# Gate and value products of three of four feed-forwards by Strassen's seven block products

## The chip, the cores and the metric

The kernel runs on one core of a Trainium2 chip. The metric is the device time in microseconds (us) of one execution. TensorE (PE) multiplies, VectorE (DVE) and ScalarE (ACT) work on tiles of 128 partitions, GpSimd (POOL) does a little, and SyncE (SP) issues the weight transfers. Each engine takes its instructions in the order in which the program lists them for it, and waits at an instruction until what it needs is there.

## The reference

The reference is a trunk of two layers on 512 tokens of 1024 features, in f32. Only the feed-forwards change:

```python
def rms_norm(x, w):
    xf = x.astype(jnp.float32)
    y = xf * lax.rsqrt(jnp.mean(xf * xf, axis=-1, keepdims=True) + EPS)
    return (y * w.astype(jnp.float32)).astype(x.dtype)

def swiglu_ffn(h, w_gu, w_down):
    a, b = jnp.split(h @ w_gu, 2, axis=-1)
    return (jax.nn.silu(a) * b) @ w_down
```

A layer adds half a feed-forward, a token mixer (layer 0: MLA and GLA in parallel, "even"; layer 1: stick-breaking attention, "odd"), half a second feed-forward, and a gated per-layer embedding ("ple": `x += sigmoid(rms_norm(x) W_g) * (p W_p)`). `w_gu` is 1024 by 2816 (gates 1408, values 1408) and `w_down` is 1408 by 1024. There are four feed-forwards: (1,0), (2,0), (1,1), (2,1), first the place in the layer, then the layer.

## The kernel before

The residual x lies in eight tiles x0 to x7 of 128 features by 512 tokens. For f32 accuracy every operand of a product is cut into a high part in a rounded 32-bit form and a low part that holds the rest, and a product is three matmuls: high by high, high by low, low by high (`mm3`, L320 to L322). A weight tile of 128 by 1024 is loaded by SP, its high part is cast on ACT (L221) and its low part subtracted on DVE (L222). `weight()` hands out weights in the order of a list (`plan`), keeps WR = 6 loads in flight and has WS = 3 of them split ahead of use.

`Norm.take(m)` follows each final residual tile: it scales the tile by the gain and splits it (L333 on ACT, L335 on DVE), squares it (L410 on ACT), and adds the square to a running sum (L419, `sqa`). `norm.sums()` has PE sum the squares over partitions (`pss`, L440), from which DVE and POOL make 1/rms (`v` L453, `rc` L455); `norm.row()` makes a row R of it for all partitions (`wide`, two matmuls, L483).

In `ffn` the weights are stationary and the 512 tokens move: each of 11 gate tiles A and 11 value tiles B is 8 k-tiles by 3 matmuls of 512 columns. `gated` (L561 to L565) multiplies by R, applies silu and multiplies, and splits the result g (L328). Then each of 8 output tiles takes 33 matmuls (`dn`) and is added to x. The first two products of a feed-forward are interleaved over k (`proj2`), so that PE meets x6 and x7 last; `norm.sums()` stands after them, `norm.row()` one product later.

A scheduler sets each engine's order at build time, from the order in which the code is written and its own estimates. It is fixed on the chip.

Of the kernel before, what the change touches and what calls it, by code (L numbers as in the profile page):

```python
# [18 lines left out]
P = 128  # L19
# [34 lines left out]
def _two_pi_parts():  # L54
    """2 pi, and 2**16 modulo 2 pi, cut into parts of 8 bits (the last one is the rest)."""
# [53 lines left out]
def tile_kernel(ctx: ExitStack, tc: tile.TileContext, a: dict, out: bass.AP):  # L109
# [156 lines left out]
    # ---- constants and inputs  # L266
# [48 lines left out]
    # ---- pieces  # L315
# [41 lines left out]
    def proj2(w0, w1, rhs, p):  # L357
        """Two products, for whose last operand there is more time."""
# [8 lines left out]
    class Filler:  # L367
        """Work for the tensor engine, to be laid between the steps of a chain."""
# [95 lines left out]
    def diagonals(cols, eng=dve):  # L464
        """Columns of tokens, in two parts, on the diagonals of blocks."""
# [13 lines left out]
    def widen(ms):  # L479
        """The diagonals as a row of the tokens on all partitions (PSUM)."""  # L480
# [12 lines left out]
    def start(norm):  # L493
        """The first two products, along with the arrival of their operands."""
# [63 lines left out]

    def gated(A, B, R, g):
# [203 lines left out]
    def values(keys, xn, done):  # L763
        """Values of 4 heads, tokens on partitions."""
# [13 lines left out]
    def even_mixer(norm, nxt, cos, sin):  # L778
# [131 lines left out]
        # decays from exact sums of the logs, of two kinds at a time  # L910
# [19 lines left out]
        # weights of the pairs within a block: [j, (block, head of the pair), i]; the diagonal first  # L930
# [23 lines left out]
        # operands of the levels; the two heads' queries stand apart, zeros in the other's rows  # L954
# [5 lines left out]
        # states between blocks  # L960
# [90 lines left out]
        # the rotated key, for the heads on either half of the quadrants  # L1051
# [162 lines left out]
    # the place of a block of keys in the banks of a head's scores, for the queries from it on  # L1214
# [3 lines left out]
    def odd_mixer(norm, nxt):  # L1218
# [32 lines left out]
        def scores(h):  # L1251
# [19 lines left out]
            # sums over the later blocks of keys  # L1271
# [100 lines left out]
    for l in range(DEPTH):  # L1372
        last = l == DEPTH - 1
        nxt = Norm(G_MIX + KD * l)
        ffn(1, l, norm, nxt, begun=begun if l == 0 else None, during=during if l == 0 else None)
        norm, nxt = nxt, Norm(G_FFN2 + KD * l)
# [6 lines left out]
        ffn(  # L1383
# [88 lines left out]
```

## Time and profile before

| | |
|---|---|
| median of 3 runs (1325.88 to 1328.06 us) | 1326.98 us |
| profiled execution: span | 1327.2 us |
| busy: PE, DVE, ACT, POOL | 1304.0, 733.5, 541.4, 138.1 us |
| mean granted TensorE clock | 0.990 |
| longest sums of PE's waits: for DVE's xnl, for DVE's mq | 6.7 us, 5.4 us |

The profiled execution's own time is its span from first to last instruction; nothing measurable lies around it, since it is 0.2 us above the median of the runs. Busy time is the time in which at least one of an engine's instructions is under way. Matmuls overlap, so a matmul's duration is longer than its distance to the next one; the distance (pitch) is what a row of them costs. The clock is a share of full speed: 1.00 is 2.4 GHz, 0.50 is 1.2 GHz.

### The profile page before, as it was taken

To read this page: it belongs to the slowest core of one execution; us is meant where nothing else is said; L and a number is where in the kernel's file an instruction comes from. 1 tells how busy PE (TensorE), PEld (TensorE's weight loads), DVE (VectorE), ACT (ScalarE), POOL (GpSimd) and SP (SyncE) were. 2 spreads that over 40 slices of the span, in tenths; PEclk is the share of its full clock that TensorE was granted. 3 is DMA by queue.
4 is the path that set the end of the run, shared out by engine and by line. 5 is a ranking of instruction groups with operands and counts; after the bars stand their busy time and mean duration, and the time that the engine had idled before them with its cause. 6 is when DMAs were issued, how large, how long until landed. Compare 5 with 4: busy or idle time off the path is not lost.

```text
span 1327.2 us, 15466 instructions
## 1 busy us (share of the span) xinstructions
PE 1304.0 (98%) x6086; PEld 1089.4 (82%) x6086; DVE 733.5 (55%) x1059; ACT 541.4 (41%) x848; POOL 138.1 (10%) x148
## 2 busy tenths in 40 slices
PE   7999999998999999999999999999999999999997
PEld 5888888887888888888888888888888888888886
DVE  6575443579865544454664444444767555444544
ACT  4333333333643333243543223334778533223442
POOL 4200000425450000000100000000111000000000
PEclk8999999998999999999999999999999999999999
DMA  7432233112301232233333223322113023323411
GB/s 237 124 96 75 85 126 106 50 44 66 109 1 48 96 95 81 83 112 113 91 108 96 86 69 100 128 95 96 64 64 97 15 84 108 96 76 103 140 47 63
DMA packets 38008, 118.59 MB, mean 89 GB/s; under 512 B 4455, under 2 KB 5608, under 8 KB 37936
## 3 DMA queue, kind: packets, MB, share of 16 engines
q1 hardware_dynamic: 36576, 114.64, 27.6%
q0 software_dynamic: 640, 1.89, 0.5%
q8 instruction: 47, 0.77, 0.2%
q10 hardware_dynamic: 720, 1.09, 0.2%
q14 instruction: 25, 0.20, 0.1%
HBM read 115.50 MB, written 2.10 MB: 89 GB/s over the span
## 4 chain that ended last, share of the span: by engine, by line
PE 92%; DVE 4%; issue 1%; ACT 1%; POOL 0%; POOLq 0%
PE A L321 6%; PE A L322 6%; PE A L320 6%; PE dn L320 6%; PE dn L321 6%; PE dn L322 6%; PE B L321 6%; PE B L320 6%; PE B L322 5%; PE sqk L320 2%; PE sqk L322 2%; PE sqk L321 2%; PE val L773 2%; PE val L775 2%; PE val L774 2%
## 5 line engine op out<-in xcount | busy, mean ns | idle before, releaser
L221 ACT CAST wh<-wr 128x1024 fp32r<-128x1024 f32 (+3 forms) x223 | 211.2, 949 | 546.9 <-issue 197.5
L222 DVE TENSOR_TENSOR wl<-wr,wh 128x1024 fp32r<-128x1024 f32 (+3 forms) x223 | 251.9, 1132 | 138.2 <-ACT wh L221 137.9
L321 PE MATMUL A<-xnl,wh 128*128 128x512 f32 x376 | 148.3, 394 | 6.7 <-DVE xnl L335 6.7
L320 PE MATMUL A<-xnh,wh 128*128 128x512 f32 x376 | 148.3, 394 | 0.1
L322 PE MATMUL A<-xnh,wl 128*128 128x512 f32 x376 | 147.6, 393 | 0.0
L320 PE MATMUL dn<-gh,wh 128*128 128x512 f32 x352 | 137.0, 389 | 0.0
L322 PE MATMUL dn<-gh,wl 128*128 128x512 f32 x352 | 137.0, 389 | 0.0
L321 PE MATMUL dn<-gl,wh 128*128 128x512 f32 x352 | 136.9, 389 | 0.0
L320 PE MATMUL B<-xnh,wh 128*128 128x512 f32 x328 | 128.3, 391 | 0.0
L322 PE MATMUL B<-xnh,wl 128*128 128x512 f32 x328 | 128.2, 391 | 0.0
L321 PE MATMUL B<-xnl,wh 128*128 128x512 f32 x328 | 128.2, 391 | 0.0
L321 PEld LDWEIGHTS A<-xnl,wh 128*128 128x128 f32 x376 | 71.3, 190 | 24.4 <-DVE xnl L335 10.0
L564 DVE TENSOR_TENSOR bb<-B,R 128x512 f32<-128x512 f32 x41 | 28.3, 690 | 108.3 <-PE B L322 108.3
L455 POOL TENSOR_TENSOR rc<-v,half 128x4 f32<-128x4 f32 x8 | 11.9, 1486 | 713.4 <-DVE v L453 713.4
L320 PEld LDWEIGHTS A<-xnh,wh 128*128 128x128 f32 x376 | 71.3, 190 | 15.7 <-ACT wh L221 0.8
L322 PEld LDWEIGHTS A<-xnh,wl 128*128 128x128 f32 x376 | 71.2, 189 | 14.6
L322 PEld LDWEIGHTS dn<-gh,wl 128*128 128x128 f32 x352 | 66.1, 188 | 13.8
L320 PEld LDWEIGHTS dn<-gh,wh 128*128 128x128 f32 x352 | 66.1, 188 | 13.7
L321 PEld LDWEIGHTS dn<-gl,wh 128*128 128x128 f32 x352 | 66.1, 188 | 13.6
L321 PEld LDWEIGHTS B<-xnl,wh 128*128 128x128 f32 x328 | 62.0, 189 | 13.0
L322 PEld LDWEIGHTS B<-xnh,wl 128*128 128x128 f32 x328 | 61.9, 189 | 13.0
L320 PEld LDWEIGHTS B<-xnh,wh 128*128 128x128 f32 x328 | 61.9, 189 | 13.0
(380 smaller groups left out, 2501.5 us busy)
## 6 DMA issues: line engine op xcount, KB each, us to landing
wr<-in_gu SPq DMA_DIRECT2D x86, 512.0 KB, 3.5
wr<-in_dn SPq DMA_DIRECT2D x32, 384.0 KB, 3.0
wr<-in_dn SPq DMA_DIRECT2D x32, 320.0 KB, 2.9
wr<-in_od_qk SPq DMA_DIRECT2D x16, 512.0 KB, 3.2
wr<-in_ev_in SPq DMA_DIRECT2D x12, 512.0 KB, 3.5
wr<-in_ev_out SPq DMA_DIRECT2D x8, 512.0 KB, 3.7
wr<-in_pg SPq DMA_DIRECT2D x8, 512.0 KB, 3.2
wr<-in_od_v SPq DMA_DIRECT2D x8, 512.0 KB, 3.2
```

The costliest lines, as they stand in the source:

```text
L221: act.copy(hi[:, cs], t[:, cs])
L222: dve.tensor_tensor(lo[:, cs], t[:, cs], f32(hi)[:, cs], op=ALU.subtract)
L320: pe.matmul(acc, wh, xh, start=start, stop=False, **k)
L321: pe.matmul(acc, wh, xl, start=False, stop=False, **k)
L322: pe.matmul(acc, wl, xh, start=False, stop=stop, **k)
L455: pool.tensor_tensor(r, v, half[:, :n], op=ALU.pow)
L564: dve.tensor_mul(b, B, R)
L773: pe.matmul(accs[b], xn[k][0][:, bs], wh[:, ws], start=k == 0, stop=False)
L774: pe.matmul(accs[b], xn[k][0][:, bs], wl[:, ws], start=False, stop=False)
L775: pe.matmul(accs[b], xn[k][1][:, bs], wh[:, ws], start=False, stop=k == KD - 1)
```

## The change

Three feed-forwards, all but (1,0), take `ffn7` and `Norm7`. Tokens are cut into two halves of 256, features into even and odd tiles, and the columns of `w_gu` into gates and values; so h @ w_gu is a product of 2 by 2 blocks, done with seven block products in place of eight. It goes in three groups of columns (512, 512 and 384 of the gates, with the same of the values). In a group each product is 24 matmuls: 2 blocks of 128 tokens, 4 k-tiles, 3 parts. The activations are stationary and the weights move, as many columns as the group has.

- **Weights.** The raw blocks of a group are 8 loads of 128 by 1024 (128 by 768 in the third). Four of the seven products need a difference of blocks: `w_term` subtracts in place on DVE (L268), 8 subtractions a group, and each of the 14 halves ("units") is then split as before (cast on ACT L247, subtraction on DVE L248). WS is 4, WR is 8 for grouped weights and 5 for others.
- **Activations.** `Norm7.take` makes the same differences of the normed activations: for an even tile two scaled copies on ACT, one subtraction of 256 tokens on DVE (`nv`, L504) and a split; for an odd tile a scaled split (`no`), `nu` (L513, L514), `nw` (L515), a split of `nu` and one of half `nw` (L521). The squares and their sum stay (now L462, L471).
- **After the products.** The sums (`al`, `be`, `ga` in PSUM, two banks each) are copied by ACT and added by DVE (`add`, L693). `close` applies silu with 1/rms as a scale per token (tokens lie on partitions now) and multiplies (L699). PE turns each of the 11 result tiles back with 4 transposes of 128 by 128 (`turn`, `gT`), and they are split. R and `wide` are not made.
- **Order.** `norm.sums()` is called after the first product (B11), ahead of the second (B21).

```diff
+        if by_seven(w, l):
+            for g in range(len(GROUPS)):
+                plan.extend(("sg", w, l, g, t, u) for t in TERMS for u in range(2))
+        else:
...
+    loads, needs, done = [], [], []
+    base, grouped = {}, set()
+    for key in plan:
+        over = done[-1] if done else 0
+        if key[0] != "sg":
+            loads.append(source(key))
+            needs.append(len(loads))
+            done.append(over + 1)
+            continue
+        g = key[:4]
+        if g not in base:
+            base[g] = len(loads)
+            grouped.update(range(len(loads), len(loads) + 8))
+            _, w_, l_, g_ = g
+            n = 2 * GROUPS[g_]
+            src = a[f"sg{w_}"][l_, g_] if GROUPS[g_] == S else a[f"sh{w_}"][l_]
+            loads.extend((src[b, u], n) for b in range(4) for u in range(2))
+        needs.append(base[g] + LAST_NEED[key[4]] * 2 + key[5] + 1)
+        done.append(over + FREED.get(key[4], 0))
...
+    def w_term(key):
+        _, _, _, _, term, u = key
+        b0 = base[key[:4]]
+        (b11, n), (b21, _), (b12, _), (b22, _) = [raw.get(b0 + 2 * b + u, (None, 0)) for b in range(4)]
+        sub = lambda o, x, y: dve.tensor_tensor(o[:, :n], x[:, :n], y[:, :n], op=ALU.subtract)
+        if term == "T1":
+            sub(b11, b12, b11)
+        elif term == "T2":
+            sub(b11, b22, b11)
+        elif term == "T3":
+            sub(b12, b22, b12)
+        elif term == "T4":
+            sub(b21, b21, b11)
+        return {"B11": b11, "B21": b21, "T1": b11, "T2": b11, "B22": b22, "T3": b12, "T4": b21}[term], n
...
+        if plan[i][0] == "sg":
+            t, n = w_term(plan[i])
+            ready[i] = w_tiles()
+            w_cut(t, n, *ready[i], slice(0, n))
+            at[1] += 1
+            return
...
-        while at[0] < min(at[2] + 1 + WR, len(plan)):
-            w_load()
-        while at[1] < min(at[0], at[2] + WS):
-            w_split()
+        while True:
+            of = done[at[1] - 1] if at[1] else 0
+            if at[0] < len(loads) and at[0] - of < (WR if at[0] in grouped else WR_PLAIN):
+                w_load()
+            elif at[1] < len(plan) and at[1] < at[2] + WS and needs[at[1]] <= at[0]:
+                w_split()
+            else:
+                break
...
+    class Norm7(Norm):
+        def __init__(self, col):
+            super().__init__(col)
+            self.even, self.odd, self.both, self.last = [], [], [], []
+            self.kept = None
+        def take(self, m, eng=dve):
+            g = gain(self.col + m)
+            lo, hi = slice(0, H), slice(H, S)
+            if m % 2 == 0:
+                v, e = sl("nv"), sl("ne")
+                act.activation(v[:, lo], x[m][:, lo], AF.Copy, scale=g)
+                act.activation(e[:, lo], x[m][:, hi], AF.Copy, scale=g)
+                dve.tensor_tensor(v[:, hi], v[:, lo], e[:, lo], op=ALU.subtract)
+                self.even.append(split(v, "nv"))
+                self.kept = v, e
+            else:
+                self.odd.append(split_scaled(x[m], g, "no"))
+                v, e = self.kept
+                u, w = sl("nu"), self.w if m % 4 == 3 else sl("nw")
+                self.w = w
+                ws = hi if m % 4 == 3 else lo
+                dve.scalar_tensor_tensor(u[:, lo], x[m][:, hi], g, e[:, lo], op0=ALU.mult, op1=ALU.add)
+                dve.tensor_tensor(u[:, hi], u[:, lo], v[:, lo], op=ALU.subtract)
+                dve.scalar_tensor_tensor(w[:, ws], x[m][:, lo], g, u[:, hi], op0=ALU.mult, op1=ALU.subtract)
+                self.both.append(split(u, "nu"))
+                if m % 4 == 1:
+                    self.last.append((sl("nwh", F32R), sl("nwl", F32R)))
+                h, l = self.last[-1]
+                act.copy(h[:, ws], w[:, ws])
+                dve.tensor_tensor(l[:, ws], w[:, ws], f32(h)[:, ws], op=ALU.subtract)
+            self.square(m, eng)
+        def side(self, term, j):
+            if term in ("B11", "T3"):
+                return self.even[j], H * (term == "T3")
+            if term in ("B21", "T4"):
+                return self.odd[j], H * (term == "T4")
+            if term in ("T1", "T2"):
+                return self.both[j], H * (term == "T2")
+            return self.last[j // 2], H * (j % 2)
...
+    def ffn7(w, l, norm, nxt, during=None, after=None):
+        g, turning = [], []
+        def product(accs, gi, term, first, last):
+            n = GROUPS[gi]
+            units = [weight("sg", w, l, gi, term, u) for u in range(2)]
+            for t in range(2):
+                for j in range(KD // 2):
+                    (h, lw), c = norm.side(term, j)
+                    cs = slice(c + t * P, c + t * P + P)
+                    wh, wl = units[j // 2]
+                    ws = slice((j % 2) * n, (j % 2) * n + n)
+                    o = accs[t][:, :n]
+                    begin, end = first and j == 0, last and j == KD // 2 - 1
+                    pe.matmul(o, h[:, cs], wh[:, ws], start=begin, stop=False, skip_group_check=True)
+                    pe.matmul(o, h[:, cs], wl[:, ws], start=False, stop=False, skip_group_check=True)
+                    pe.matmul(o, lw[:, cs], wh[:, ws], start=False, stop=end, skip_group_check=True)
+        def turn(count):
+            for _ in range(min(count, len(turning))):
+                tiles, i = turning.pop(0)
+                pt = bank("gT")
+                for b in range(NB):
+                    pe.transpose(pt[:, b * P : b * P + P], tiles[b][:, i * P : i * P + P], ident)
+                g.append(split(pt, "g"))
+        def copies(accs, n):
+            out_ = [sl("r") for _ in range(2)]
+            for t in range(2):
+                act.copy(out_[t][:, :n], accs[t][:, :n])
+            return out_
+        def add(tiles, accs, n):
+            for t in range(2):
+                dve.tensor_tensor(tiles[t][:, :n], accs[t][:, :n], tiles[t][:, :n], op=ALU.add)
+        def close(c, o, srcs, b0, n):
+            for t in range(2):
+                r = rc[:, b0 + t : b0 + t + 1]
+                act.activation(c[t][:, :n], srcs[t][:, :n], AF.Silu, scale=r)
+                dve.scalar_tensor_tensor(o[t][:, :n], o[t][:, :n], r, c[t][:, :n], op0=ALU.mult, op1=ALU.mult)
+        for gi, n in enumerate(GROUPS):
+            two = lambda name: [bank(name) for _ in range(2)]
+            al = two("al")
+            product(al, gi, "B11", True, False)
+            if gi == 0:
+                rc = norm.sums()
+            c11 = copies(al, n)
+            turn(2)
+            be = two("be")
+            product(be, gi, "B21", True, True)
+            add(c11, be, n)
+            turn(2)
+            ga = two("ga")
+            product(ga, gi, "T1", True, False)
+            c22 = copies(ga, n)
+            product(al, gi, "T2", False, False)
+            c12 = copies(al, n)
+            product(ga, gi, "B22", False, True)
+            add(c12, ga, n)
+            close(c11, c12, c11, 0, n)
+            product(al, gi, "T3", False, False)
+            add(c22, al, n)
+            product(al, gi, "T4", False, True)
+            s2 = [sl("r") for _ in range(2)]
+            close(s2, c22, al, 2, n)
+            turning.extend(([*c12, *c22], i) for i in range(n // P))
...
+        cut = DN[0] // P
+        early = KF - GROUPS[-1] // P
+        accs = [bank("dn"), None]
+        part(accs[0], weight("dn", w, l, 0, 0), 0, cut, 0)
+        w01 = weight("dn", w, l, 0, 1)
+        part(accs[0], w01, cut, early, cut)
+        turn(2)
+        accs[1] = bank("dn")
+        part(accs[1], weight("dn", w, l, 1, 0), 0, cut, 0)
+        turn(2)
+        part(accs[0], w01, early, KF, cut)
...
-        ffn(1, l, norm, nxt, begun=begun if l == 0 else None, during=during if l == 0 else None)
-        norm, nxt = nxt, Norm(G_FFN2 + KD * l)
+        if by_seven(1, l):
+            ffn7(1, l, norm, nxt)
+        else:
+            ffn(1, l, norm, nxt, begun=begun if l == 0 else None, during=during if l == 0 else None)
+        norm, nxt = nxt, Norm7(G_FFN2 + KD * l)
         if l % 2 == 0:
             even_mixer(norm, nxt, *tables)
         else:
             odd_mixer(norm, nxt)
         norm, nxt = nxt, Norm(G_PLE + KD * l)
         pT = []
-        ffn(
+        ffn7(
...
-            norm, nxt = nxt, Norm(G_FFN1 + KD * (l + 1))
+            norm, nxt = nxt, Norm7(G_FFN1 + KD * (l + 1))
...
-NSLAB = 66
-WR = 6
-WS = 3
+NSLAB = 64
+WR = 8
+WR_PLAIN = 5
+WS = 4
...
+GROUPS = (512, 512, 384)
+TERMS = ("B11", "B21", "T1", "T2", "B22", "T3", "T4")
+LAST_NEED = {"B11": 0, "B21": 1, "T1": 2, "T2": 3, "B22": 3, "T3": 3, "T4": 3}
+FREED = {"T3": 2, "T4": 2}
...
+def by_seven(w, l):
+    return (w, l) != (1, 0)
```

The first place is PE's program at the start of feed-forward (2,0), where `nvh`, `nvl` are the parts of the even tiles, `noh`, `nol` those of the odd ones, `wh`, `wl` those of a weight, and `pss` the squares' sums. After the change it reads:

```order
L673 MATMUL al_3687<-wh_3596,nvh_3631 128x512
L674 MATMUL al_3687<-wl_3597,nvh_3631 128x512
L673 MATMUL al_3688<-wh_3596,nvh_3631 128x512
L674 MATMUL al_3688<-wl_3597,nvh_3631 128x512
L675 MATMUL al_3687<-wh_3596,nvl_3633 128x512
L675 MATMUL al_3688<-wh_3596,nvl_3633 128x512
L538 MATMUL pss_3722<-ones,sqa_3685 128x2
L538 MATMUL pss_3722<-ones,sqa_3685 128x2 x3
L673 MATMUL be_3735<-wh_3639,noh_3412 128x512
```

Before, PE's rows at the same place were these:

```order
L322 MATMUL A_3647<-xnh_3565,wl_3576 128x512
L320 MATMUL A_3625<-xnh_3605,wh_3535 128x512
L321 MATMUL A_3625<-xnl_3607,wh_3535 128x512
L322 MATMUL A_3625<-xnh_3605,wl_3536 128x512
L320 MATMUL A_3647<-xnh_3605,wh_3575 128x512
L321 MATMUL A_3647<-xnl_3607,wh_3575 128x512
L322 MATMUL A_3647<-xnh_3605,wl_3576 128x512
L440 MATMUL pss_3675<-ones,sqa_3611 128x2
L440 MATMUL pss_3675<-ones,sqa_3611 128x2 x3
L320 MATMUL A_3690<-xnh_3383,wh_3615 128x512
```

`pss` stood after two products (A_3625, A_3647) and now stands after one (al_3687 and al_3688 are the two token blocks of B11), ahead of all of B21.

The second place is DVE's program that leads to that `pss`: the last twelve rows up to the last sum of squares (`sqa_3685`, which `pss` reads; x7 is x_79). After:

```order
L380 TENSOR_TENSOR nvl_3633<-nv_3626,nvh_3631 128x512
L268 TENSOR_TENSOR wr_2692<-wr_2692,wr_2688 128x1024
L471 TENSOR_TENSOR sqa_3637<-sqa_3594,sq_3635 128x512
L248 TENSOR_TENSOR wl_3739<-wr_2690,wh_3738 128x1024
L387 SCALAR_TENSOR_TENSOR nol_3671<-x_79,gains,noh_3669 128x512
L513 SCALAR_TENSOR_TENSOR nu_3673<-x_79,gains,ne_3627 128x256
L268 TENSOR_TENSOR wr_2690<-wr_3504,wr_2690 128x1024
L514 TENSOR_TENSOR nu_3673<-nu_3673,nv_3626 128x256
L268 TENSOR_TENSOR wr_3297<-wr_3297,wr_2690 128x1024
L515 SCALAR_TENSOR_TENSOR nw_3580<-x_79,gains,nu_3673 128x256
L380 TENSOR_TENSOR nul_3679<-nu_3673,nuh_3677 128x512
L471 TENSOR_TENSOR sqa_3685<-sqa_3637,sq_3683 128x512
```

Before, the last rows up to `sqa_3611` were these, two whole tiles of the residual:

```order
L488 TENSOR_TENSOR x_78<-x_78,eo_3539 128x512
L222 TENSOR_TENSOR wl_3576<-wr_3413,wh_3575 128x1024
L335 SCALAR_TENSOR_TENSOR xnl_3567<-x_78,gains,xnh_3565 128x512
L419 TENSOR_TENSOR sqa_3571<-sqa_3531,sq_3569 128x512
L488 TENSOR_TENSOR x_79<-x_79,eo_3579 128x512
L222 TENSOR_TENSOR wl_3616<-wr_3453,wh_3615 128x1024
L335 SCALAR_TENSOR_TENSOR xnl_3607<-x_79,gains,xnh_3605 128x512
L419 TENSOR_TENSOR sqa_3611<-sqa_3571,sq_3609 128x512
```

Between the last residual and the last square there were 2 rows; now there are 18, with four weight subtractions (L268) and three weight splits (L248) among them. From the residual of x3 (x_75) to the last square DVE has 50 rows: 15 of 1024 columns (7 splits, 8 subtractions), 18 of 512 with two tiles, 3 of 512 with a gain, and 14 of 256. At the start of (2,1) there are likewise 50 from the residual of x4: 11, 18, 3 and 18.

The third place is ACT's program ahead of feed-forward (1,1), in the ple of layer 0, where `gt` of L794 is the sigmoid of a tile:

```order
L247 CAST wh_5545<-wr_5121 128x1024
L794 ACTIVATE gt_5418<-gt_5418 128x512
L502 ACTIVATE nv_5423<-x_76,gains 128x256
L503 ACTIVATE ne_5424<-x_76,gains 128x256
L247 CAST wh_5599<-wr_5168 128x1024
L378 CAST nvh_5428<-nv_5423 128x512
L462 ACTIVATE sq_5432<-x_76 128x512
L247 CAST wh_5604<-wr_5117 128x1024
L794 ACTIVATE gt_5472<-gt_5472 128x512
```

The casts of weights, which wait for PE to release a buffer, stand among the links of the chain of x4 (x_76) and x5. DVE's program from the first `gt` of this ple to the last square has 74 rows: 17 of 1024 (9 splits, 8 subtractions), 34 of 512 with two tiles, 4 of 512 with a gain, 19 of 256.

## Rows read from the trace of the kernel before

**Rows 1.** The page's first part: busy time by engine, share of the span, instructions.

```profile
PE 1304.0 (98%) x6086; PEld 1089.4 (82%) x6086; DVE 733.5 (55%) x1059; ACT 541.4 (41%) x848; POOL 138.1 (10%) x148
```

**Rows 2.** The page's chain that ended last, by engine.

```profile
PE 92%; DVE 4%; issue 1%; ACT 1%; POOL 0%; POOLq 0%
```

**Rows 3.** PE's waits: engine, line and waited for; total us, times, longest.

```profile
PE A L321 <- DVE xnl L335: 6.7, 5, 2.6
PE pa L1030 <- DVE mq L1021: 5.4, 3, 3.0
```

**Rows 4.** Windows: us, busy PE PEld DVE ACT POOL (instructions), clock, DMA share, GB/s.

```profile
446.00:624.00 178.00, 178.00 (x791) 147.44 (x790) 87.56 (x112) 60.45 (x80) 1.94 (x1) 1.00 0.32 101
...
416.00:456.00 40.00, 40.00 (x182) 33.19 (x181) 19.96 (x29) 14.29 (x18) 1.94 (x1) 1.00 0.28 93
640.00:686.00 46.00, 46.00 (x209) 38.20 (x208) 31.95 (x41) 22.19 (x32) 9.70 (x6) 1.00 0.25 80
1058.00:1095.00 37.00, 37.00 (x169) 30.75 (x168) 23.46 (x35) 16.41 (x23) 1.94 (x1) 1.00 0.25 76
```

**Rows 5.** PE's timeline, products of 512 columns; start and duration in us.

```profile
458.24 0.39 PE L320 MATMUL A<-xnh,wh 128*128 128x512 f32 x1
...
463.68 0.39 PE L320 MATMUL B<-xnh,wh 128*128 128x512 f32 x1
```

**Rows 6.** PE's timeline, matmuls of 384 columns in the even mixer.

```profile
365.28 0.33 PE L320 MATMUL sc<-krh,qrh 128*128 128x384 f32 x1
...
365.80 0.22 PE L1116 MATMUL sc<-cr 128*128 128x128 f32 x1
```

**Rows 7.** Transposes: PE's timeline, then the tile's durations (ns, least/mean/most).

```profile
1230.92 2.04 PE L608 MATMUL xt<-ident,x 128*128 128x128 f32 x16
1232.71 0.48 PE L320 MATMUL dn<-gh,wh 128*128 128x512 f32 x1
...
L608 PE MATMUL xt<-ident,x x32: 272/273/327, 1230.9 to 1283.5; 128*128 128x128 f32 x32
```

**Rows 8.** DVE's timeline ahead of feed-forward (2,0).

```profile
414.32 1.23 DVE L222 TENSOR_TENSOR wl<-wr,wh 128x1024 fp32r<-128x1024 f32 x1 [0.17 <-ACT wh L221]
415.46 0.75 DVE L335 SCALAR_TENSOR_TENSOR xnl<-x,gains,xnh 128x512 fp32r<-128x512 f32 x1
416.13 0.68 DVE L419 TENSOR_TENSOR sqa<-sqa,sq 128x512 f32<-128x512 f32 x1
...
446.89 0.16 DVE L453 TENSOR_SCALAR v<-pss 128x4 f32<-128x4 f32 x1 [8.27 <-PE pss L440]
```

**Rows 9.** DVE's timeline in the ple of layer 0, first and last tile.

```profile
635.47 0.68 DVE L595 TENSOR_TENSOR gt<-G,R 128x512 f32<-128x512 f32 x1
636.85 0.69 DVE L597 TENSOR_TENSOR gt<-gt,J 128x512 f32<-128x512 f32 x1 [0.70 <-ACT gt L596]
...
672.83 0.68 DVE L595 TENSOR_TENSOR gt<-G,R 128x512 f32<-128x512 f32 x1
673.43 1.22 DVE L222 TENSOR_TENSOR wl<-wr,wh 128x1024 fp32r<-128x1024 f32 x1
...
676.77 0.75 DVE L335 SCALAR_TENSOR_TENSOR xnl<-x,gains,xnh 128x512 fp32r<-128x512 f32 x1 [0.79 <-ACT xnh L333]
```

**Rows 10.** PE's timeline there: end of `wide`, and the first product of (1,1).

```profile
633.74 0.40 PE L320 MATMUL G<-xnh,wh 128*128 128x512 f32 x1
...
671.86 0.39 PE L320 MATMUL A<-xnh,wh 128*128 128x512 f32 x1
```

**Rows 11.** DVE groups by shape: busy us, mean ns, idle before.

```profile
L1269 DVE SCALAR_TENSOR_TENSOR u<-z,u 128x256 f32<-128x256 f32 x8 | 3.4, 420 | 1.6 <-ACT u L1267 1.6
L222 DVE TENSOR_TENSOR wl<-wr,wh 128x1024 fp32r<-128x1024 f32 x149 | 185.3, 1245 | 91.8 <-ACT wh L221 91.5
```

**Rows 12.** Windows across the even mixer's wait of PE; columns as in Rows 4.

```profile
312.00:318.00 6.00, 1.90 (x12) 1.27 (x10) 5.91 (x5) 0.00 (x0) 5.51 (x5) 0.95 0.00 0
318.00:324.00 6.00, 5.85 (x18) 4.98 (x19) 5.39 (x14) 2.23 (x4) 1.29 (x1) 0.50 0.17 59
```

More of the change, by code (lines that the diff above doesn't have):

```diff
@@ L140, in ffn_plan @@
     def ffn_plan(w, l):
-        for f in range(KF):
-            plan.append(("gu", w, l, f))
-            plan.append(("gu", w, l, KF + f))
+        if by_seven(w, l):
+            for g in range(len(GROUPS)):
+                plan.extend(("sg", w, l, g, t, u) for t in TERMS for u in range(2))
+        else:
+            for f in range(KF):
+                plan.append(("gu", w, l, f))
+                plan.append(("gu", w, l, KF + f))
         for m in range(KD):
@@ L235, in wc @@
         return w[o // S][:, o % S : o % S + P] if isinstance(w, list) else w[:, o : o + P]
+    def w_term(key):
[12 more added lines that the diff above has]
+        return {"B11": b11, "B21": b21, "T1": b11, "T2": b11, "B22": b22, "T3": b12, "T4": b21}[term], n
     def w_split():
         i = at[1]
-        t, n = raw.pop(i)
+        if plan[i][0] == "sg":
[4 more added lines that the diff above has]
+            return
+        t, n = raw.pop(needs[i] - 1)
         if kept(i):
@@ L253, in weight @@
         assert plan[at[2]] == key, (plan[at[2]], key)
-        while at[0] < min(at[2] + 1 + WR, len(plan)):
-            w_load()
-        while at[1] < min(at[0], at[2] + WS):
-            w_split()
+        while True:
[6 more added lines that the diff above has]
+                break
         k = plan[min(at[1], len(plan) - 1)][0]
         for _ in range(BURST.get(k, 0)):
-            if at[1] < min(at[0], at[2] + AHEAD) and kept(at[1]):
+            if at[1] < at[2] + AHEAD and at[1] < len(plan) and needs[at[1]] <= at[0] and kept(at[1]):
                 w_split()
@@ L555, in ffn, with part @@
             residual(m, acc, 0.5, nxt)
+            if after and m in after:
+                after[m]()
+    def ffn7(w, l, norm, nxt, during=None, after=None):
[60 more added lines that the diff above has]
+            turning.extend(([*c12, *c22], i) for i in range(n // P))
+        if during:
+            during()
+        def part(acc, wt, k0, k1, c0):
+            wh, wl = wt
+            for kk in range(k0, k1):
+                o = slice((kk - c0) * P, (kk - c0) * P + P)
+                mm3(acc, wh[:, o], wl[:, o], g[kk][0], g[kk][1], kk == 0, kk == KF - 1)
+        cut = DN[0] // P
[9 more added lines that the diff above has]
+        part(accs[0], w01, early, KF, cut)
+        for m in range(KD):
+            if m > 1:
+                accs.append(bank("dn"))
+                part(accs[m], weight("dn", w, l, m, 0), 0, cut, 0)
+            if m > 0:
+                part(accs[m], weight("dn", w, l, m, 1), cut, KF, cut)
+            residual(m, accs[m], 0.5, nxt)
@@ L1387, in tile_kernel @@
             nxt,
-            during={KF - 1: lambda: pT.extend(load_p(l))},
+            during=lambda: pT.extend(load_p(l)),
             after={3: lambda: turn_x(0, xt)} if last else None,
@@ L1421, in _layout, with groups @@
     )
+    o["gu1"] = _tiles(i["ffn1_w_gu"][0])[None]
+    def groups(w, c0, n):
+        w = w.reshape(KD // 2, 2, P, 2, FF)[..., c0 : c0 + n]
+        return w.reshape(2, 2, 2, P, 2, n).transpose(4, 2, 0, 3, 1, 5).reshape(4, 2, P, 2 * n)
     for f in (1, 2):
-        o[f"gu{f}"] = np.stack([_tiles(w) for w in i[f"ffn{f}_w_gu"]])
+        ws = i[f"ffn{f}_w_gu"]
+        o[f"sg{f}"] = np.stack([np.stack([groups(w, S * g, S) for g in range(2)]) for w in ws])
+        o[f"sh{f}"] = np.stack([groups(w, 2 * S, FF - 2 * S) for w in ws])
         o[f"dn{f}"] = np.stack([_tiles(w) for w in i[f"ffn{f}_w_down"]])
@@ L1452, in build @@
     import concourse.bacc as bacc
-    nc = bacc.Bacc("TRN2", target_bir_lowering=False, num_devices=1)
+    nc = bacc.Bacc("TRN2", target_bir_lowering=False, num_devices=1, dynamic_dma_scratch_size=4096)
     a = {
```

3 lines of the change are left out of this document (2 added, 1 removed).

## The prediction

> **What bounds the kernel now.** I read the busy times first: PE is busy 1304.0 of 1327.2 us, DVE 55% and ACT 41% of the span [rows 1]. Then the chain that ended last: 92% of it is PE, 4% DVE [rows 2]. Then PE's waits: the two longest sums are 6.7 and 5.4 us [rows 3]. So TensorE bounds the kernel, and a matmul taken away is worth its pitch, as long as nothing else makes PE wait. Then windows: in feed-forward (2,0) PE is busy in all of 178 us at clock 1.00, while DVE is busy in 87.56 and ACT in 60.45; and at the starts of the three feed-forwards that the change touches PE does not wait either, while DVE is busy 19.96 of 40, 31.95 of 46 and 23.46 of 37 us [rows 4]. So none of the waits of [rows 3] is there to be won back, and the reserve that the change draws on is DVE's.
>
> **PE, products.** From the first matmul of one product to the first of the next is 463.68 − 458.24 = 5.44 us for 24 matmuls of 512 columns, 0.2267 each [rows 5]. Three matmuls of 384 columns take 365.80 − 365.28 = 0.52, 0.173 each [rows 6], so a shorter moving side pays in proportion, with stationary operands that are new each time. A feed-forward has 22 × 24 = 528 of the first kind for gates and values: 119.7 us. After, two groups of 7 × 24 = 168 take 76.2, the third, of 384 columns, 29.1; together 105.3. That is −14.4 a feed-forward. The two `wide` matmuls go: −0.45.
>
> **PE, turning back.** 11 tiles by 4 transposes are added. 16 transposes took 1.79 us from the first to the matmul behind them, 0.112 each, though each lasts 272 ns by itself [rows 7], since they overlap. 44 × 0.112 = +4.9. The net is −14.4 − 0.45 + 4.9 = −9.9 (unrounded), three times −29.8. This alone would give 1297.4.
>
> **DVE and ACT within the groups.** DVE has 14 splits and 8 subtractions of 1024 columns in a group of 512, 10 operations of 512 with two tiles and 4 with a scale. The distances on DVE are 415.46 − 414.32 = 1.14 and 416.13 − 415.46 = 0.67 [rows 8], and 0.60 from the last `gt` to the next row [rows 9]; so 25.1 + 6.0 + 2.7 = 33.8 us, against PE's 7 × 5.44 + 16 × 0.112 = 39.9. It fits, at 85%. I cost it at nothing; cover gone, it would cost what the third rival says. The weights' bytes are unchanged, so transfers (0.32 of the engines busy [rows 4]) stay hidden.
>
> **The starts.** Here the reserve is too small. `pss` stands in PE's program ahead of all of B21, needs the last sum of squares, and everything on PE is queued behind it. Before, DVE had two rows between the last residual and that sum and then waited 8.27 us for `pss` [rows 8]. Now PE comes there one product earlier, and DVE has the additions of `Norm7` and the first group's subtractions and splits in its queue ahead of it. I sum DVE's queue at these distances, with 0.34 for 256 columns (420 ns [rows 11] less the 0.08 by which 512 columns follow closer than their 0.68 [rows 9]).
>
> (2,0): x3 becomes final at 0, x7 four products later at 21.8, and B11 ends at 27.2. DVE's 50 rows from there on are 15 × 1.14 + 18 × 0.60 + 3 × 0.67 + 14 × 0.34 = 34.7. At least 7.5 us of waiting.
>
> (1,1): from the end of `wide` PE needs 671.86 − 633.74 = 38.1 to the feed-forward [rows 10], and 43.6 to the end of B11. DVE starts 1.7 after `wide` [rows 9, 10] and has 74 rows: 17 × 1.14 + 34 × 0.60 + 4 × 0.67 + 19 × 0.34 = 48.9, done at 50.7. At least 7.1.
>
> (2,1): from x4's residual three products and B11, 21.8. DVE's 50 rows: 11 × 1.14 + 18 × 0.60 + 3 × 0.67 + 18 × 0.34 = 31.5. At least 9.7.
>
> These 24.3 us are a floor: DVE never waits in them. It will. In the ple each tile's sigmoid costs DVE a wait of 0.70 for ACT, and each scaled copy 0.79 [rows 9]; before, they fell in DVE's spare time. Eight tiles: 11.9. And the last two tiles of each start are a chain through ACT (the copies `nv` and `ne`, `nvh`, `noh`, `nuh`), while the split of a later unit also waits for PE to let go of B11's second unit: five hand-overs at 0.70, 3.5 a start. So 11.0, 22.5 and 13.2: 46.7 us. The other end is from durations in place of distances (1.245 [rows 11], 0.68, 0.75 [rows 8, 9], 0.42): 39.1, 55.3 and 35.7 for the three queues, 15.1 us more. I take 46.7, since DVE runs these rows back to back, where distances count.
>
> **The clock.** In the one place where PE idled for about 4 us, its granted clock in the next 6 us was 0.50, the level of 1.2 GHz [rows 12]. 5.85 us of work at half speed lose 2.9. I take 2.0 for each start, 6.0 in all, with 0 and 8.8 as ends.
>
> **Sum.** 1327.2 − 29.8 + 46.7 + 6.0 = 1350.1. The profiled execution stands 0.2 above the median of 1326.98, which I leave out: 1350 us, 1.7% slower.
>
> **The rivals.**
> *DVE keeps ahead.* If the last square is ready when PE ends B11, the gain stays whole: 1297, faster. For it: DVE idles 2 us or more of every product of the mixers' ends now, and was 8.27 us early [rows 8]. Against it: the sums above overrun without a single wait of DVE. It decides from the point at which the three starts' waits and the slow clock behind them together are under 27 us (0.2%, 2.7 us, is about what a measurement of this kernel can tell from no change).
> *The floor alone.* DVE runs without hand-overs: 24.3, and 0 to 6 for the clock: 1322 to 1328, at the edge between faster and the same. It wants ACT never to be late, while ACT gets the `Norm7` copies as well, and casts that wait for PE stand ahead of the sigmoids in its queue.
> *DVE becomes the bound in all groups too.* If ten hand-overs of 0.79 in a group are not hidden, DVE needs 33.8 + 7.9 = 41.7 against 39.9: 1.8 in each of six groups, and in the third ones about 31.3 against 30.4, 0.9 each: 14 us more, 1364. For it: 85% on an engine that waits in order. Against it: four units are split ahead, a margin of about two products.
> *Transposes cost their duration.* 132 × 0.272 = 35.9 in place of 14.8 [rows 7]: 21 more, 1371. Against it is the row itself: the matmul behind the sixteen starts 1.79 us after the first, and no idle time stands ahead of it. The Trainium skill, page "TensorE: Matmul & The Clock Gate", section "Part 4: PE-mode transpose", gives about 275 ns for a 128 by 128 transpose in a kernel's context and says that the full clock doesn't engage for transposes. The trace agrees with the 275 as a duration (272) but not as a price.
>
> **How the numbers follow.** The forecast, waits of 36 to 60 us, gets 0.62 (its own range is 1338 to 1364); a smaller overrun (1328 to 1338) 0.06; the floor 0.10, half of it faster and half the same; DVE ahead 0.06; DVE bound in the groups 0.13; transposes 0.03. Faster is 0.06 + 0.05 = 0.11, the same 0.06 (the other half of the floor and what touches it), slower 0.83. The range reaches down into the floor, 1325, and up to 1368, the sum with the upper ends of the starts and of the clock (1327.2 − 29.8 + 61.8 + 8.8 = 1368.0); some 0.10 is left out below and 0.07 above.
>
> **What would show it.** Right: PE waits at L538 `pss` for DVE `sqa`, three times, 7 us or more each, the longest ahead of (1,1); shorter waits for `nvl` (L675) just ahead of it; DVE nearly full in the 30 to 50 us before; clock below 1.00 behind each wait; and PE full from B21 on to the end of each feed-forward, with 5.44 us a product and about 0.45 for four transposes. Wrong: no wait at `pss`; or waits of PE in the middle of groups for `wl` of L248; or transposes at 0.27. The forecast fails above all if DVE's queue runs without its hand-overs to ACT.

## The result, and the profile after

The changed kernel takes 1355.49 us (median of 4 runs, 1353.65 to 1356.53) against 1327.52 for the kernel before beside it: a ratio of 1.0216, 95% interval 1.0204 to 1.0229. It is slower by 2.2%; the forecast was 1350, range 1325 to 1368. A run's time stands above its span, by 1.8 to 3.5 us in all runs listed here (1356.53 and 1354.5 for the profiled one), so it does not hold that nothing measurable lies around the span. The prediction's sum starts from a span; its 1350.1 is therefore to be held against 1354.5.

The page of the profile after, where it answers to [rows 1, 2]: PE has 16 us less work, DVE 147 more, the span is 1354.5 us, the mean clock 0.971.

```profile
PE 1288.4 (95%) x6140; PEld 1088.7 (80%) x6140; DVE 880.9 (65%) x1242; ACT 639.4 (47%) x1010; POOL 136.9 (10%) x148
...
PE 88%; DVE 8%; ACT 2%; issue 1%; POOL 0%; POOLq 0%; DVEq 0%; ACTq 0%
```

PE's waits after, beside [rows 3]:

```profile
PE al L673 <- ACT nvh L378: 23.5, 4, 12.1
PE pss L538 <- DVE sqa L471: 17.6, 3, 7.7
...
PE al L675 <- DVE nvl L380: 1.1, 1, 1.1
```

42.2 us in eight waits, all of them between the start of a feed-forward and its `pss`. PE's timeline of the three starts (start and duration, then in brackets the idle time ahead):

```profile
435.12 0.39 PE L673 MATMUL al<-wh,nvh 128*128 128x512 f32 x1
...
442.07 0.50 PE L673 MATMUL al<-wh,nvh 128*128 128x512 f32 x1 [2.70 <-ACT nvh L378]
...
452.04 1.87 PE L538 MATMUL pss<-ones,sqa 128*128 128x2 f32 x8 [7.66 <-DVE sqa L471]
...
675.98 0.39 PE L673 MATMUL al<-wh,nvh 128*128 128x512 f32 x1
...
680.72 0.50 PE L675 MATMUL al<-wh,nvl 128*128 128x512 f32 x1 [1.12 <-DVE nvl L380]
694.04 0.80 PE L673 MATMUL al<-wh,nvh 128*128 128x512 f32 x1 [12.12 <-ACT nvh L378]
704.63 1.87 PE L538 MATMUL pss<-ones,sqa 128*128 128x2 f32 x8 [7.66 <-DVE sqa L471]
...
1099.76 0.39 PE L673 MATMUL al<-wh,nvh 128*128 128x512 f32 x1
...
1104.30 0.50 PE L673 MATMUL al<-wh,nvh 128*128 128x512 f32 x1 [1.65 <-ACT nvh L378]
1113.43 0.79 PE L673 MATMUL al<-wh,nvh 128*128 128x512 f32 x1 [7.05 <-ACT nvh L378]
1118.59 1.87 PE L538 MATMUL pss<-ones,sqa 128*128 128x2 f32 x8 [2.23 <-DVE sqa L471]
```

Undisturbed, `pss` would stand 5.44 us after the first `al`. It came 11.5, 23.2 and 13.4 us after that: 48.1 in all, of which 42.2 idle and the rest matmuls of B11 at half clock. ACT is named as the releaser of the first matmul that reads x6: it casts `nvh` from `nv`, which DVE makes. DVE's timeline at (2,0), from the residual of x3 to the last square, shows the queue that the prediction summed, with 2.2 us of idle time in 37.6:

```profile
414.35 0.68 DVE L586 TENSOR_TENSOR x<-x,eo 128x512 f32<-128x512 f32 x1
...
430.94 0.68 DVE L586 TENSOR_TENSOR x<-x,eo 128x512 f32<-128x512 f32 x1
...
439.81 1.23 DVE L248 TENSOR_TENSOR wl<-wr,wh 128x1024 fp32r<-128x1024 f32 x1 [0.85 <-ACT wh L247]
440.95 0.42 DVE L504 TENSOR_TENSOR nv<-nv,ne 128x256 f32<-128x256 f32 x1
441.28 1.22 DVE L268 TENSOR_TENSOR wr<-wr,wr 128x1024 f32<-128x1024 f32 x1
...
451.30 0.69 DVE L471 TENSOR_TENSOR sqa<-sqa,sq 128x512 f32<-128x512 f32 x1
```

The residual of x6 was final at 431.6, and `nv` of x6 began at 440.95. Weight splits and subtractions stood ahead of it on DVE, but ACT was late too: its two copies of x6, which `nv` reads, ended at 440.58, behind a weight cast that had waited for PE.

```profile
438.73 1.05 ACT L247 CAST wh<-wr 128x1024 fp32r<-128x1024 f32 x1 [1.21 <-PE al L675]
439.68 0.50 ACT L502 ACTIVATE nv<-x,gains 128x256 f32<-128x256 f32 x1
440.09 0.49 ACT L503 ACTIVATE ne<-x,gains 128x256 f32<-128x256 f32 x1
```

So the 2.70 us ahead of x6 are not DVE's alone. With DVE's order as it is, ACT's lateness can have moved the last square at (2,0) by no more than DVE's idle time, 2.2 of the 37.6 us.

The clock (windows, columns as in [rows 4]): 0.50 while PE waits, and still 0.50 for the first matmuls behind `pss`.

```profile
444.00:452.00 8.00, 0.38 (x1) 0.00 (x0) 7.35 (x12) 4.01 (x7) 0.00 (x0) 0.50 0.00 0
...
454.00:456.00 2.00, 2.00 (x5) 1.57 (x6) 0.11 (x1) 0.00 (x0) 1.01 (x1) 0.50 0.00 0
456.00:458.00 2.00, 2.00 (x8) 1.60 (x7) 0.00 (x0) 0.00 (x0) 0.00 (x0) 0.79 0.00 0
458.00:460.00 2.00, 2.00 (x10) 1.65 (x9) 0.69 (x1) 0.93 (x1) 0.00 (x0) 1.00 0.00 0
```

By stretches the balance closes. From one stage's first matmul to the next's, (2,0) became 4.0 us longer, (1,1) 15.8, (2,1) 7.1, together 26.9 of the spans' 27.3. With 9.9 won in each, 13.9, 25.7 and 17.0 were lost; 48.1 of these 56.6 stand ahead of `pss`, the other 8.5 are slow clock behind it (from its first matmul to the next product's, B21 took 6.99, 6.99 and 8.15 us in place of 5.44, and `pss` is longer too).

### The profile page after: what moved, and what is told of

It reads as the page before. It is cut to its first block, busy times and chain, and to the rows that moved or that the text cites. A ratio compares the mean times of both kernels' runs of the same rounds, so it can differ in the third digit from the quotient of the medians.

```text
span 1354.5 us, 15990 instructions
## 1 busy us (share of the span) xinstructions
PE 1288.4 (95%) x6140; PEld 1088.7 (80%) x6140; DVE 880.9 (65%) x1242; ACT 639.4 (47%) x1010; POOL 136.9 (10%) x148
## 4 chain that ended last, share of the span: by engine, by line
PE 88%; DVE 8%; ACT 2%; issue 1%; POOL 0%; POOLq 0%; DVEq 0%; ACTq 0%
PE dn L374 6%; PE dn L373 6%; PE dn L372 6%; PE al L675 4%; PE al L673 4%; PE al L674 4%; PE ga L673 2%; PE ga L675 2%; PE ga L674 2%; PE sqk L372 2%; PE sqk L374 2%; PE sqk L373 2%; PE val L971 2%; PE val L972 2%; PE val L973 2%; PE A L373 1%
## 5 line engine op out<-in xcount | busy, mean ns | idle before, releaser
L247 ACT CAST wh<-wr 128x1024 fp32r<-128x1024 f32 (+3 forms) x283 | 264.9, 938 | 418.6 <-PE dn L373 79.7
L248 DVE TENSOR_TENSOR wl<-wr,wh 128x1024 fp32r<-128x1024 f32 (+3 forms) x283 | 314.0, 1112 | 188.0 <-ACT wh L247 187.2
L268 DVE TENSOR_TENSOR wr<-wr,wr 128x1024 f32<-128x1024 f32 (+1 forms) x72 | 80.9, 1138 | 0.1
L673 PE MATMUL al<-wh,nvh 128*128 128x512 f32 (+1 forms) x144 | 55.1, 383 | 23.5 <-ACT nvh L378 23.5
L372 PEld LDWEIGHTS dn<-gh,wh 128*128 128x128 f32 x352 | 66.1, 188 | 13.4
L675 PE MATMUL al<-wh,nvl 128*128 128x512 f32 (+1 forms) x144 | 55.0, 384 | 1.3 <-DVE nvl L380 1.1
L674 PE MATMUL al<-wl,nvh 128*128 128x512 f32 (+1 forms) x144 | 54.3, 378 | 0.0
L372 PE MATMUL sqk<-xnh,wh 128*128 128x512 f32 x128 | 50.3, 393 | 0.0
L374 PE MATMUL sqk<-xnh,wl 128*128 128x512 f32 x128 | 50.0, 391 | 0.0
L373 PE MATMUL sqk<-xnl,wh 128*128 128x512 f32 x128 | 50.0, 390 | 0.0
L373 PE MATMUL A<-xnl,wh 128*128 128x512 f32 x88 | 36.0, 409 | 6.3 <-DVE xnl L387 6.3
L971 PE MATMUL val<-wh,xnh 128*128 128x512 f32 x96 | 37.6, 392 | 0.0
```

Of the source, the lines that this page charges most:

```text
L247: act.copy(hi[:, cs], t[:, cs])
L248: dve.tensor_tensor(lo[:, cs], t[:, cs], f32(hi)[:, cs], op=ALU.subtract)
L268: sub = lambda o, x, y: dve.tensor_tensor(o[:, :n], x[:, :n], y[:, :n], op=ALU.subtract)
L372: pe.matmul(acc, wh, xh, start=start, stop=False, **k)
L373: pe.matmul(acc, wh, xl, start=False, stop=False, **k)
L374: pe.matmul(acc, wl, xh, start=False, stop=stop, **k)
```

## The experiments

The theory: DVE's in-order queue is too long in the 30 to 60 us ahead of each first product, and `pss`, put ahead of B21, makes PE wait for its last entry. The rivals: only the place of `pss`; ACT's queue; DVE short of time everywhere. Every kernel is the changed one with the edit shown; line numbers shift by a few. Ratios are to the kernel before (95% intervals).

**One start less.** Feed-forward (1,1) and the norm ahead of it as before the change.

```diff
-            norm, nxt = nxt, Norm7(G_FFN1 + KD * (l + 1))
+            norm, nxt = nxt, Norm(G_FFN1 + KD * (l + 1))
...
-    return (w, l) != (1, 0)
+    return w == 2
```

> The changed kernel, with feed-forward (1,1) as before the change (and the plain norm ahead of it); (2,0) and (2,1) stay by seven products. Theory (each start costs by itself): (1,1) was 15.8 us longer than before the change (9.9 won, 20.9 waited, the rest slow clock), so 1355.5 - 15.8 = about 1340. Rival (the cost lies in things common to all three, loads and buffers): the loss halves or less, 1345 to 1350.

1337.62 us (1.0092, 1.0070 to 1.0113), 17.9 less. The waits at the other two starts stayed as they were (2.70, 7.66; 1.66, 7.05, 2.23). Each start costs by itself.

**The sums later.**

```diff
             product(al, gi, "B11", True, False)
-            if gi == 0:
-                rc = norm.sums()
...
             product(ga, gi, "B22", False, True)
+            if gi == 0:
+                rc = norm.sums()
```

> The sums of squares over partitions are asked for after the fifth product (B22) and no longer after the first; DVE's work is the same. Theory (DVE's queue is late, PE idles only because its next work stands behind it): x7's last part still comes at the same time, but PE fills the wait with B21 and most of T1; the three waits shrink from 42.2 us to about 17 (1, 13, 2) and the slow clock behind them from 14.5 to about 5: about 1320 us. Rival 1 (the place of the sums is the whole cause): only the waits at the sums go, 17.6 us, with their clock: about 1333. Rival 2 (DVE has no reserve left, the wait moves on to the weights' splits of T1 and T2): 1345 to 1355.

1324.78 us (0.9981, 0.9971 to 0.9991): 31 us from one moved call. The waits at the starts are 0.9, 9.5 and 6.0, 16.4 in all; DVE's work is unchanged (876.6 us busy). With `pss` out of the way the scheduler put half to three quarters of B21 ahead of B11's last k-tile, and the first matmuls of T1 ahead of B21's last, so more than the waits at `pss` went: the first rival's 1333 is passed. The largest part of what is left lies at (1,1), behind the ple:

```profile
672.53 0.50 PE L673 MATMUL be<-wh,noh 128*128 128x512 f32 x1 [1.76 <-ACT noh L385]
678.76 0.79 PE L673 MATMUL ga<-wh,nuh 128*128 128x512 f32 x1 [3.71 <-DVE gt L793]
690.63 0.63 PE L673 MATMUL be<-wh,noh 128*128 128x512 f32 x1 [3.68 <-ACT noh L385]
```

**Less in DVE's queue.** The first group's subtractions are pinned in program order, behind the split traced just before them. In DVE's order one of them stays ahead of the last square at each start; the others are behind it.

```diff
-        sub = lambda o, x, y: dve.tensor_tensor(o[:, :n], x[:, :n], y[:, :n], op=ALU.subtract)
+        held = tc.keep_in_program_order if key[3] == 0 else lambda i: i
+        sub = lambda o, x, y: held(dve.tensor_tensor(o[:, :n], x[:, :n], y[:, :n], op=ALU.subtract))
```

> The eight weight subtractions of each first group are kept behind the last sum of squares in DVE's order; the sums stay after the first product. Theory: 9.1, 9.1 and 6.8 us of subtractions and the two or three splits that hang on them leave DVE's queue ahead of the sums; waits fall from 10.4, 20.9 and 10.9 to about 1, 11 and 4, the clock's loss to about 5: about 1320 us, and no new wait of PE at the splits of T1. Rival (the subtractions filled gaps of DVE, which waits for ACT and PE anyway): 1350 to 1355. Rival (T1's weights come late instead): waits of 3 to 5 us appear ahead of T1 in each of the three: about 1335.

1337.16 us (1.0075, 1.0058 to 1.0092): 18 less than the changed kernel, where 35 was expected. The waits are 2.7, 15.9 and 7.5, against 1, 11 and 4. The direction holds, so the subtractions did not merely fill gaps; but in the ple they partly did. There DVE's last rows now wait for ACT link by link:

```profile
679.63 0.43 DVE L505 TENSOR_TENSOR nv<-nv,ne 128x256 f32<-128x256 f32 x1 [1.11 <-ACT ne L504]
680.74 0.69 DVE L381 TENSOR_TENSOR nvl<-nv,nvh 128x512 fp32r<-128x512 f32 x1 [0.69 <-ACT nvh L379]
...
683.33 0.69 DVE L796 TENSOR_TENSOR gt<-gt,J 128x512 f32<-128x512 f32 x1 [0.70 <-ACT gt L795]
```

The `nol` of x7 waits 0.79 us for `noh` in the same way. No wait of PE appeared ahead of T1.

**The subtractions on POOL.**

```diff
-        sub = lambda o, x, y: dve.tensor_tensor(o[:, :n], x[:, :n], y[:, :n], op=ALU.subtract)
+        sub = lambda o, x, y: pool.tensor_tensor(o[:, :n], x[:, :n], y[:, :n], op=ALU.subtract)
```

> All weight subtractions go to POOL, which does 512 columns of two tiles in about 1.5 us, so some 3 us each, 24 of a group's 40. ACT's order is as it was. Theory (DVE's queue): 9.1, 9.1, 6.8 us less on DVE; if POOL doesn't slow DVE, about 1325 us. If DVE's instructions are lengthened while POOL runs (one of 1.14 took 1.7 in the ple), much of it is lost: 1335 to 1360. Rival (ACT's casts that wait for PE hold up nvh, DVE does not matter): no change, 1355, and the same waits for nvh.

1385.57 us (1.0445, 1.0428 to 1.0461), slower than any of the bounds given. DVE has 72 instructions less and is busy for longer (902.3 us against 880.9). Its rows at (2,0), then POOL's of the same time:

```profile
421.70 0.42 DVE L514 TENSOR_TENSOR nu<-nu,nv 128x256 f32<-128x256 f32 x1
422.16 2.50 DVE L515 SCALAR_TENSOR_TENSOR nw<-x,gains,nu 128x256 f32<-128x256 f32 x1
424.58 2.89 DVE L380 TENSOR_TENSOR nul<-nu,nuh 128x512 fp32r<-128x512 f32 x1
427.40 0.41 DVE L521 TENSOR_TENSOR nwl<-nw,nwh 128x256 fp32r<-128x256 f32 x1
...
421.87 5.07 POOL L268 TENSOR_TENSOR wr<-wr,wr 128x1024 f32<-128x1024 f32 x2 [28.24 <-DVE wl L248]
```

Two DVE instructions of 0.48 and 0.69 elsewhere take 2.50 and 2.89: each lasts about as long as the POOL subtraction beside it (two in 5.07 here, 2.75 us in the mean of all 48 of that size). The Trainium skill, page "SBUF — State Buffer", section "SBUF: two separate sides", says that an instruction of DVE with two inputs in SBUF and one of GpSimd that reads SBUF share a port pair, that whichever starts first holds it for the whole instruction, and that the other fully blocks. These rows agree. So the run puts more time into DVE's queue, not less. Since ACT's order was left alone and the waits grew with DVE's time (33.4 us for `nvh`, 20.7 for `sqa`), it speaks for the theory and against ACT's casts as the only cause, but it does not show what a free third engine would give.

**Both edits** (`held_late`), the sums later and the subtractions pinned.

> Both edits: subtractions of the first group behind the last square, and the sums after B22. Theory: what is left is the chain of the ple ahead of (1,1), about 6 to 10 us, and 2 us of clock: 1305 to 1312, faster than both kernels (1297 is the gain with no wait at all). Rival (DVE's backlog moves into the group): 1320 to 1335 with waits at the splits of T1 to T4.

1318.78 us (0.9942, 0.9922 to 0.9963): the theory's range is missed by 7 us. No wait of PE is left at (2,0); 9.2 us remain at (1,1) in five waits, as expected, but 2.1 at (2,1), and 3.4 in two waits for DVE's `add`, were not. These 14.8 us leave 6.7 of the 21.5 by which the kernel stands above 1297.3, the 1327.06 of the kernel before beside it less the whole gain of 29.8; these 6.7 were not taken apart. Not every subtraction had gone behind the last square: in DVE's timeline two, three and three of the eight still stand ahead of it. And one wait at (1,1) is ACT's: x6 was final at 674.67, but its copies stood behind a weight cast that waited 4.43 us for PE's T1.

```profile
676.04 1.05 ACT L247 CAST wh<-wr 128x1024 fp32r<-128x1024 f32 x1 [4.43 <-PE ga L676]
676.99 0.51 ACT L503 ACTIVATE nv<-x,gains 128x256 f32<-128x256 f32 x1
...
679.38 0.50 PE L674 MATMUL al<-wh,nvh 128*128 128x512 f32 x1 [2.74 <-ACT nvh L379]
```

**All eight subtractions behind the last square** (`behind_late`), with the sums later.

```diff
-        sub = lambda o, x, y: dve.tensor_tensor(o[:, :n], x[:, :n], y[:, :n], op=ALU.subtract)
+        def sub(o, x, y):
+            with tc.issue_after(behind[0]) if key[3] == 0 else nullcontext():
+                dve.tensor_tensor(o[:, :n], x[:, :n], y[:, :n], op=ALU.subtract)
...
-                eng.tensor_tensor(acc, self.acc, sq, op=ALU.add)
+                behind[0] = eng.tensor_tensor(acc, self.acc, sq, op=ALU.add).ins
```

> Sums after B22, and every subtraction of a first group issued behind the last sum of squares in DVE's order (held_late had kept one ahead of it at (2,0) and four at (1,1)). Theory: the four rows and the splits that hang on them, 5 to 7 us, leave DVE's queue inside the ple: PE's waits at (1,1) go from 9.2 to about 3, about 1311 us. Rival (the chain of the ple through ACT sets x7, the subtractions filled its gaps): 1317 to 1320.

1319.67 us (0.9948, 0.9931 to 0.9965), the number of the rival but not its mechanism. x7 did come earlier (5.7 us of waits for x6 and x7, from 8.7 for x5 to x7), and T1's weights became late instead, at (1,1) and at (2,1):

```profile
682.30 1.22 PE L679 MATMUL ga<-wh,nuh 128*128 128x512 f32 x2 [4.34 <-ACT wh L248]
...
1088.50 1.22 PE L679 MATMUL ga<-wh,nuh 128*128 128x512 f32 x2 [3.61 <-ACT wh L248]
```

**Also the odd tiles' `nu` and `nw` later**, behind all residual tiles (`Norm7.take` keeps them in a list, `finish()` ahead of B11 writes them).

> As behind_late, and the parts of the odd tiles that only the third to seventh products read (nu and nw, five DVE instructions and two casts for each odd tile) are written behind all residual tiles, ahead of the first product. Theory: DVE's queue ahead of x7 is 8 us shorter still, so PE does not wait ahead of B21; but these instructions now stand ahead of T1 with its four subtractions and splits, some 13 us in a row against one product of 5.4: waits of 3 to 8 us ahead of T1 in each of the three: 1315 to 1325. Rival (DVE catches up, since its queue is empty by then): 1305.

1330.66 us (1.0033, 1.0020 to 1.0046). PE no longer waits ahead of B21, and waits 5.6, 8.7 and 5.7 us ahead of T1's tiles for `nuh` and `nul`: 20 in all, 11 us slower than without this edit, and 6 above the range that was forecast. What is put off comes due one product later: this order only moves the wait.

**Only T2, T3 and T4 behind the last square.** T1's subtractions may go ahead (`and term != "T1"` in the condition above), the sums later. Then the same with (1,1) as before the change, and `held_late` likewise.

> Sums after B22; of the first group's subtractions only those of T2, T3 and T4 are issued behind the last sum of squares, T1's two may go ahead. Theory (DVE's queue has two due times: x7's parts and the sums for the first two products, T1's units for the third): T1's waits of 4.3 and 3.6 us of behind_late go, and PE's waits ahead of x6 and x7 at (1,1) come back by 2 to 3 us: about 1315, some 4 better than held_late and behind_late. Rival (nothing to win by order, DVE's total sets the start): 1318 to 1320.

1315.80 us (0.9921, 0.9909 to 0.9934). The waits for T1's weights are gone at (1,1) and (2,1), and at (2,0) PE does not wait at all. At (1,1) 6.6 us remain, the most of them ahead of T1's first matmul for a `gt` of the ple, and at (2,1) 1.6 us for T2's weights.

```profile
674.75 0.63 PE L679 MATMUL ga<-wh,nuh 128*128 128x512 f32 x1 [4.10 <-DVE gt L799]
```

> The same with feed-forward (1,1) as before the change. At (2,0) and (2,1) PE then hardly waits: held_late_two less its waits of 1.8 and 0.35 us: 1311 to 1313. Rival: no difference from held_late_two, 1314.

1311.51 us (0.9888, 0.9873 to 0.9903), the fastest kernel here that leaves nothing out.

> held_late with feed-forward (1,1) as before the change. The stretch from the first ple to the odd mixer was 430.1 us in held_late and 423.8 before the change, so 1318.8 - 6.3 = about 1312. If the gain of (1,1) were whole in held_late, it would be 1329.

1314.42 us (0.9906, 0.9892 to 0.9921). So two feed-forwards by seven products beat three in both orders tried (1314.42 against 1318.78, 1311.51 against 1315.80): (1,1) by seven products wins 9.9 us on PE and loses some 14, of which 10.9 and 6.6 are waits of PE behind the ple.

**Without 96 of the 132 transposes.**

> held_late without the transposes of the first two groups (the results are split as they lie, so the product with w_down works on other numbers): 96 of 132 transposes are left out. Theory (a transpose costs its distance, 0.10 to 0.11 us): 10 us less than held_late, 1308 to 1309. Rival (it costs its duration, 0.272): 26 less, 1293.

1307.94 us (0.9852, 0.9839 to 0.9866): 10.8 less than `held_late`, 0.113 us for each transpose.

## Why the prediction was right

**The gain on PE** (−9.9 a feed-forward, −29.8 in all) was right where it can be read by itself: at (2,0), where PE does not wait in the kernel with T2 to T4 behind, the stretch from the even mixer's output products to the ple's first product is 608.9 − 407.6 = 201.3 us, against 210.9 before the change: −9.6. The rows, the kernel before first:

```profile
L320 PE MATMUL eo<-omh,wh x20: 389/389/389, 407.8 to 431.6; 128*128 128x512 f32 x20
L320 PE MATMUL G<-xnh,wh x64: 389/389/398, 618.7 to 671.2; 128*128 128x512 f32 x64
```

```profile
L378 PE MATMUL eo<-omh,wh x20: 389/389/389, 407.6 to 431.4; 128*128 128x512 f32 x20
L378 PE MATMUL G<-xnh,wh x64: 389/389/398, 608.9 to 661.3; 128*128 128x512 f32 x64
```

**The transposes** cost their distance. The estimate was 0.112 us; eight of them took 0.79 in the changed kernel, and leaving out 96 gave 0.113 each. The 275 ns of the Trainium skill (page "TensorE: Matmul & The Clock Gate", section "Part 4: PE-mode transpose") are a duration here and no price.

```profile
493.40 1.04 PE L682 MATMUL gT<-ident,r 128*128 128x128 f32 x8
494.19 0.48 PE L673 MATMUL be<-wh,noh 128*128 128x512 f32 x1
```

**The starts** were forecast at 11.0, 22.5 and 13.2 us, 46.7, and came to 11.5, 23.2 and 13.4, 48.1. DVE's queues were forecast at 38.2 from x3's residual at (2,0), 64.3 from the first `gt` at (1,1), and 35.0 from x4's at (2,1); they took 37.6, 65.0 and 34.9. A sum of distances on an in-order queue, with a hand-over to ACT for each link of a chain, was close enough to decide the sign. That it was within 1 us is luck: DVE's idle time was 2.2, 11.4 and 1.7 us where the hand-overs had been priced at 3.5, 15.4 and 3.5, 7.1 less in all, and its rows took 35.4, 53.6 and 33.2 where 34.7, 48.9 and 31.5 had been summed, 7.1 more. Two of the rows at (1,1) were 0.5 and 1.1 us longer than others of their size, each beside a sum of squares on POOL.

**Where PE waits** was off. 7 us or more at each `pss` was forecast, with short waits just ahead; it was 7.7, 7.7 and 2.2 at `pss`, and 2.7, 13.2 and 8.7 at the parts of x4 to x6, because those stand in the same queue behind early weight work. The first of the signs named for a right prediction, 7 us at `pss` three times, came twice. The moment of `pss`, which the sum gave, did not depend on it, because `pss` needs the last entry of that queue either way.

**The clock** was mis-sized: 2.0 us a start, 6.0 in all, against 8.5 behind `pss` and nearly 6 more inside the delay ahead of it, which the 46.7 had meant as idle time. The starts (1.4 us) and the clock behind them (2.5) make up 3.9 of the 4.4 us between 1350.1 and the span of 1354.5. Held as it was worded, the sum had the idle time 4.5 too long (42.2 for 46.7) and the slow clock 8.4 too short (14.4 for 6.0).

**Within the groups** DVE has room, but little. In the kernel with both edits it is busy 35.61 of 40 us at (2,0) (89%, forecast 85%), and PE waits 0.1.

```profile
446.00:486.00 40.00, 39.89 (x188) 32.58 (x186) 35.61 (x39) 23.98 (x31) 1.01 (x1) 1.00 0.34 106
```

So DVE works off slowly what is put behind the last square, and the two reorderings that put off most, all eight subtractions or `nu` and `nw`, met a wait at T1. PE, the full engine, cannot make up a lost start at all. The rival in which DVE becomes the bound in all groups did not come.

What stays open: how much of (1,1) is DVE's load, how much the chain of hand-overs in the ple, and how much ACT's order, in which copies of the residual stand behind weight casts that wait for PE. The kernel with the subtractions pinned shows that the first two count, and the one with both edits has a wait of the third kind; no run changed ACT's order alone.

## What to carry to other kernels

A change that trades work of the full engine for work of half-empty ones has to be checked stage by stage: DVE, at 55% of the span before, still had too little room in the 30 to 60 us where the new operands come into being. Sum the in-order queue from the last fixed event to the first instruction that the full engine waits for, and give each entry a due time. A small reduction that nobody needs until later, here the sums of squares, must not stand in the full engine's program ahead of work that is ready: moving that one call, with the new order that the scheduler then made, was worth 31 us.

## What the runs showed of the hardware

Two DVE instructions that read two tiles took about as long as the POOL instruction beside them, 2.50 and 2.89 us in place of 0.48 and 0.69. And short waits can cost clock too: at (2,1) of the fastest kernel PE did the small matmuls of `pss` (0.95 us), waited 1.10, did two matmuls and waited 0.53. The granted clock, 1.00 up to 1088, was 0.50 in the 2 us from 1090 on, with PE busy throughout, and 0.89 in the mean of the 16 us around.

```profile
1084.36 0.95 PE L544 MATMUL pss<-ones,sqa 128*128 128x2 f32 x8
1086.41 0.73 PE L679 MATMUL al<-wh,nuh 128*128 128x512 f32 x2 [1.10 <-ACT wh L248]
1087.67 0.50 PE L680 MATMUL al<-wl,nuh 128*128 128x512 f32 x1 [0.53 <-DVE wl L249]
...
1084.00:1090.00 6.00, 4.37 (x21) 3.26 (x20) 6.00 (x8) 3.51 (x6) 0.00 (x0) 0.89 0.00 0
1090.00:1092.00 2.00, 2.00 (x6) 1.62 (x5) 2.00 (x2) 2.00 (x3) 0.00 (x0) 0.50 0.00 0
...
1090.00:1100.00 10.00, 10.00 (x41) 8.15 (x40) 9.68 (x10) 7.01 (x9) 1.02 (x1) 0.89 0.48 188
```
